# A planned ten-stage transformer kernel: the norms' reciprocal roots move from VectorE chains to two GpSimd instructions each

## Chip, cores and metric

One core of a Trainium2 chip. The time is the device time of one launch in microseconds (us), the median of several runs. TensorE is the matmul engine (PE), VectorE is DVE, ScalarE is ACT, GpSimd is POOL; SyncE (SP) issues nearly all DMAs.

## The reference

Two blocks follow each other on x of 256 rows x 1024 columns, all in float32. Each has two layers. In outline:

```python
def _rmsnorm(x, g):  # over 1024 columns
    y = x * rsqrt(mean(x * x, -1) + EPS)
    return y * g
def _swiglu(x, wg, wu, wd):  # d_ff = 2816
    return (silu(x @ wg) * (x @ wu)) @ wd
# first block, layers 0 (even) and 1 (odd):
x = x + 0.5 * _rmsnorm(_swiglu(_rmsnorm(x, g[0]), ...), g[1])
x = x + _rmsnorm(mixer(_rmsnorm(x, g[2])), g[3])
x = x + 0.5 * _rmsnorm(_swiglu(_rmsnorm(x, g[4]), ...), g[5])
# mixer of layer 0: conv module (31 taps, layer norm) and banded attention; of layer 1: forgetting attention
# second block:
h = x + mlstm_mixer(rmsnorm(x))        # rsqrt of the mean square per head inside
h = h + swiglu(rmsnorm(h))
kv = rmsnorm(h) @ w_kv
h = h + chunked_relpos_attention(rmsnorm(h), kv)
h = h + swiglu(rmsnorm(h))
return rmsnorm(h, final_norm_g)
```

## The kernel before

The ten stages are called F1 (feed-forward), even, F3, F4, fox, F6, ml, F8, rel, F10, and then `final`. x stays in SBUF as two tiles of 128 rows, b0 and b1. All weights (295 MB of loads in all) stream from HBM once, in "units" of 128 x 2048 floats. Each is split by ACT (high part, rounded) and DVE (low part, the rest) into two tiles of the matmul's type, tag `hl`; a product is three matmuls (high x high, high x low, low x high), method `mm3`. Four of the feed-forward stages pair some chunks after Strassen, with additions on DVE.

A norm ahead of a stage (`norm`) multiplies x by the gain on DVE, transposes it on TensorE through PSUM (`split_T`: ACT copies the high half, DVE subtracts for the low half, tag `xt`), and squares x on ACT with a sum over the columns (`ssq`). The root scales the product only afterwards, when its PSUM bank is evacuated. A post-norm (`postnorm`, six stages) squares the accumulator on ACT, takes the product with the gain on DVE, and needs the root before x is updated; the next stage's norm begins with that x.

The root is `rstd`: a chain on DVE that starts from an integer guess and does three Newton steps on a column of 128 x 1 (128 x 4 for the mLSTM heads). It is called 20 times for norms ahead of a projection (with `more=True`, which adds half the root), 12 times for post-norms, twice for the conv's layer norm, four times for the mLSTM heads. `cut=3` lets the planner put other work between its steps. The final norm's two roots go through `pow`: two GpSimd instructions.

All operations are recorded first (`Rec`), each with an assumed duration and a key. `schedule` is a planner inside the program: it picks for each engine the ready operation with the smallest key, hands out tile buffers of a fixed count per tag, and so fixes the order in each queue. `NUDGE` is a table of corrections to the keys, one entry for each labelled group of operations (" p" for its matmuls); it is where the work order is set. DMA loads are ordered in the same way; the first ones (constants, x, the four pieces of weight unit 0) have negative keys. Profile lines name the helper that records the operation: L213 `act`, L223 `tt`, L233 `ts`, L242 `stt`, L293 `mm`, L298 `tr`, L302 `load`, L271 and L273 `pow`.

Of the kernel before, what the change touches and what calls it, by code (L numbers as in the profile page):

```python
# [8 lines left out]
I32 = mybir.dt.int32  # L9
AF = mybir.ActivationFunctionType  # L10
# [66 lines left out]
class Rec:  # L77
# [189 lines left out]
    def pow(self, s, a, b, key=None):  # L267

        v, y, e = s[:, 0:1], s[:, 1:2], s[:, 2:3]
        self.op("POOL", 350, [a, b], [v],  # L270
                lambda: self.nc.gpsimd.tensor_scalar(self.res(v), self.res(a), self.res(b), EPS, ALU.add, ALU.add), key=key)  # L271
        self.op("POOL", 600, [v, e], [y],
                lambda: self.nc.gpsimd.tensor_tensor(self.res(y), self.res(v), self.res(e), ALU.pow), key=key)  # L273
        return y
# [25 lines left out]
    def load(self, out, src, nbytes, key=None, after=None):  # L300
        o = self.op("DMA", max(nbytes / (360.0 if key > 0 else 250.0), 453.0), [src], [out],
                    lambda: self.nc.sync.dma_start(self.res(out), self.res(src)),  # L302
                    lat=4000.0 if nbytes >= 400000 and out.v.name[:3] != "raw" else 2000.0, key=key)
        if after is not None:
            o.deps.append(after)
            after.succ.append(o)
            o.soft = after
        return o
# [180 lines left out]
class Net:  # L489
# [12 lines left out]
    def consts(self):  # L502
# [3 lines left out]
        w = r.t("s", name="warm")  # L506
        r.memset(w[:, 0:1], 0.0, key=-40)
# [6 lines left out]
        for b in range(2):  # L514
            x = r.t("x", name=f"x{b}")
            for h in range(2):
                r.load(x[:, h * 512:(h + 1) * 512], a["x"][b * P:(b + 1) * P, h * 512:(h + 1) * 512], P * 2048, key=-30 + 0.15 * b + 0.75 * h)
            self.x.append(x)
# [60 lines left out]
    def rstd(self, ss, w, n, key, more=False, cut=1):  # L579

        r = self.r
        s = r.t("s", name="rs")
        v, vh, y, t = s[:, 0:w], s[:, w:2 * w], s[:, 2 * w:3 * w], s[:, 3 * w:4 * w]
        r.begin()
        r.ts(v, ss[0], 1.0 / n, EPS, ALU.mult, ALU.add)
        if len(ss) > 1:
            r.end(key)
            r.begin()
            r.stt(v, ss[1], 1.0 / n, v, ALU.mult, ALU.add)
        r.ts(y.bitcast(I32), v.bitcast(I32), -0.5, 1597463007.0, ALU.mult, ALU.add)  # L590
        r.ts(vh, v, -0.5, None, ALU.mult)
        for i in range(3):
            if w == 1:
                r.stt(t, y, vh, y, ALU.mult, ALU.mult)
            else:
                r.tt(t, y, y, ALU.mult)
                r.tt(t, t, vh, ALU.mult)
            r.stt(y, t, 1.5, y, ALU.add, ALU.mult)
            if cut > 1 and i < 2:
                r.end(key)  # L600
                r.begin()
        if more:
            r.stt(s[:, 5:6], y, 0.5, y, ALU.mult, ALU.mult)
            r.ts(s[:, 4:5], y, 0.5, None, ALU.mult)
        r.end(key)
        if more:
            return y, s[:, 4:5], s[:, 5:6]
        return y
# [16 lines left out]
    def ssq(self, b, key):  # L625
# [3 lines left out]
        for h in range(2):  # L629
            junk = r.t("b2", name="junk")  # L630
            r.act(junk[:, :], self.x[b][:, h * 512:(h + 1) * 512], AF.Square, accum=ss[:, h:h + 1], key=key)
# [82 lines left out]
    def postnorm(self, b, acc, g, scale):  # L714
# [5 lines left out]
        for h in range(2):  # L720
            sl = slice(h * 512, h * 512 + 512)
            junk = r.t("b2", name="junk")
            r.act(junk[:, :], acc[h][:, :], AF.Square, accum=ss[:, h:h + 1], key=key)
# [896 lines left out]
    def final(self, gi):  # L1620
        r = self.r
        g = self.gain(gi, self.u - 5)
        for b in range(2):
# [7 lines left out]
            s = r.t("s", name="rs")  # L1631
            r.memset(s[:, 2:3], -0.5, key=key - 40)
            r.tt(y[:, 512:], self.x[b][:, 512:], g[:, 512:], ALU.mult, key=key)
            rs = r.pow(s, ss[:, 0:1], ss[:, 1:2], key=key)
# [26 lines left out]
def arrange(i):  # L1661
# [276 lines left out]
```

## Time and profile before

| | |
|---|---|
| median of 3 runs | 1586.29 us (1584.86 to 1587.45) |
| profiled execution | 1587.08 us, span from first to last instruction 1585.3 us |
| mean granted TensorE clock | 0.997 |
| TensorE busy | 1548.6 us |
| DVE, ACT, GpSimd busy | 1217.4, 938.1, 1.9 us |
| loads and stores | 296.92 MB, 187 GB/s over the span |

A matmul group's busy time counts pipelined instructions that overlap, so the place where TensorE loses time is read from its idle gaps and its granted clock, not from the mean of an instruction.

### The profile page before, as it was taken

To read this page: it belongs to the slowest core of one execution; us is meant where nothing else is said; L and a number is where in the kernel's file an instruction comes from. 1 tells how busy PE (TensorE), PEld (TensorE's weight loads), DVE (VectorE), ACT (ScalarE), POOL (GpSimd) and SP (SyncE) were. 2 spreads that over 40 slices of the span, in tenths; PEclk is the share of its full clock that TensorE was granted. 3 is DMA by queue.
4 is the path that set the end of the run, shared out by engine and by line. 5 is a ranking of instruction groups with operands and counts; after the bars stand their busy time and mean duration, and the time that the engine had idled before them with its cause. 6 is when DMAs were issued, how large, how long until landed. Compare 5 with 4: busy or idle time off the path is not lost.

```text
span 1585.3 us, 21242 instructions
## 1 busy us (share of the span) xinstructions
PE 1548.6 (98%) x7546; PEld 1266.6 (80%) x7546; DVE 1217.4 (77%) x2137; ACT 938.1 (59%) x1480; POOL 1.9 (0%) x8
## 2 busy tenths in 40 slices
PE   8999999999999999999999999999999999999998
PEld 6888878788887888787787887788877887788886
DVE  6555689798878869776899687898788674788784
ACT  6444545865555656456875565656566566765562
POOL 0000000000000000000000000000000000000000
PEclk9999999999999999999999999999999999999999
DMA  8556466447474475643664475455463755464560
GB/s 329 199 186 210 164 219 222 136 169 232 146 269 156 152 242 166 223 155 125 208 207 166 168 259 196 130 184 188 158 212 134 245 174 178 165 216 149 188 231 35
DMA packets 86779, 296.92 MB, mean 187 GB/s; under 512 B 9552, under 2 KB 13072, under 8 KB 86672
## 3 DMA queue, kind: packets, MB, share of 16 engines
q1 hardware_dynamic: 86384, 295.03, 55.1%
q8 instruction: 59, 0.97, 0.2%
q10 hardware_dynamic: 288, 0.52, 0.1%
q14 instruction: 48, 0.39, 0.1%
HBM read 294.44 MB, written 1.08 MB: 186 GB/s over the span
## 4 chain that ended last, share of the span: by engine, by line
PE 90%; DVE 6%; ACT 1%; issue 1%; DMA 1%; SPq 0%; POOLq 0%; POOL 0%; DVEq 0%; ACTq 0%
PE mm L293 59%; PE acc L293 27%; PE mm L298 4%; DVE hl L223 1%; DVE b L242 1%; DVE s L242 1%; ACT b L213 1%; DVE b L223 1%; DMA b<-in_w 1%; DVE x L242 1%; DMA x<-in_x 0%; DVE xt L223 0%; DVE s L233 0%; DVE b L254 0%; ACT L213 0%
## 5 line engine op out<-in xcount | busy, mean ns | idle before, releaser
L293 PE MATMUL mm<-hl,xt 128*128 128x512 f32 (+1 forms) x4104 | 983.6, 393 | 5.6 <-DVE xt L223 1.9
L293 PEld LDWEIGHTS mm<-hl,xt 128*128 128x128 f32 x4104 | 758.1, 188 | 168.7 <-DVE xt L223 4.8
L223 DVE TENSOR_TENSOR hl<-b,hl 128x1024 fp32r<-128x1024 f32 (+1 forms) x554 | 660.7, 1212 | 147.5 <-PE mm L293 70.5
L213 ACT ACTIVATE hl<-b 128x1024 fp32r<-128x1024 f32 (+1 forms) x554 | 572.5, 1052 | 325.4 <-PE mm L293 196.3
L293 PE MATMUL acc<-hl,gt 128*128 128x512 f32 x1584 | 385.7, 393 | 1.2 <-DVE gt L223 0.7
L293 PEld LDWEIGHTS acc<-hl,gt 128*128 128x128 f32 x1584 | 296.8, 189 | 63.9 <-DVE gt L223 1.9
L213 ACT ACTIVATE b<-mm,s 128x256 f32<-128x256 f32 (+2 forms) x150 | 77.3, 520 | 157.6 <-PE mm L293 151.1
L223 DVE TENSOR_TENSOR b<-b,b 128x1024 f32<-128x1024 f32 (+2 forms) x112 | 116.8, 1057 | 10.9 <-DMA b<-in_w 10.1
L298 PE MATMUL mm<-cst,b 128*128 128x128 f32 (+1 forms) x648 | 96.2, 276 | 9.7 <-DVE b L223 4.3
L298 PEld LDWEIGHTS mm<-cst,b 128*128 128x128 f32 (+1 forms) x648 | 77.5, 141 | 32.7 <-DVE b L223 7.0
L242 DVE SCALAR_TENSOR_TENSOR b<-mm,s,b 128x256 f32<-128x256 f32 x102 | 48.9, 479 | 63.2 <-ACT b L213 62.9
L293 PE MATMUL acc<-hl,xt 128*128 128x512 f32 x384 | 93.2, 395 | 0.9 <-DVE hl L223 0.9
L213 ACT ACTIVATE b<-b,s 128x256 f32<-128x256 f32 (+2 forms) x184 | 77.8, 450 | 24.9 <-DVE b L223 14.9
L293 PEld LDWEIGHTS acc<-hl,xt 128*128 128x128 f32 x384 | 70.6, 188 | 17.3 <-DVE hl L223 1.3
L223 DVE TENSOR_TENSOR gt<-mm,gt 128x512 fp32r<-128x512 f32 (+1 forms) x72 | 46.1, 642 | 32.7 <-ACT gt L213 32.4
L213 ACT ACTIVATE gt<-mm 128x512 fp32r<-128x512 f32 (+1 forms) x72 | 39.7, 553 | 41.7 <-PE mm L298 37.8
L213 ACT ACTIVATE b<-mm 128x512 f32<-128x512 f32 (+3 forms) x84 | 45.2, 546 | 13.8 <-PE mm L298 10.7
L242 DVE SCALAR_TENSOR_TENSOR s<-s 128x1 f32<-128x1 f32 (+2 forms) x248 | 45.4, 183 | 7.4
L213 ACT ACTIVATE b<-x 128x512 f32<-128x512 f32 x44 | 27.5, 627 | 25.8 <-DVE x L223 12.4
L242 DVE SCALAR_TENSOR_TENSOR hl<-b,cst,hl 128x512 fp32r<-128x512 f32 x48 | 33.1, 745 | 7.7 <-issue 7.6
L213 ACT ACTIVATE hl<-b,cst 128x512 fp32r<-128x512 f32 x48 | 32.7, 719 | 4.1 <-PE mm L293 3.3
L213 ACT ACTIVATE xt<-mm 128x512 fp32r<-128x512 f32 x40 | 23.4, 593 | 15.8 <-PE mm L298 14.9
(79 smaller groups left out, 597.9 us busy)
## 6 DMA issues: line engine op xcount, KB each, us to landing
b<-in_w SPq DMA_DIRECT2D x512, 512.0 KB, 5.1
g<-in_gains SPq DMA_DIRECT2D x16, 512.0 KB, 6.8
b<-in_diag SPq DMA_DIRECT2D x8, 512.0 KB, 4.6
b<-dr SPq DMA_DIRECT2D x16, 256.0 KB, 5.7
g<-in_relb SPq DMA_DIRECT2D x4, 512.0 KB, 4.7
b<-in_diag SPq DMA_DIRECT2D x4, 448.0 KB, 7.9
x<-in_x SPq DMA_DIRECT2D x4, 256.0 KB, 2.8
b<-in_w SPq DMA_DIRECT2D x4, 256.0 KB, 6.0
```

The costliest lines, as they stand in the source:

```text
L213: return self.nc.scalar.activation(self.res(out), self.res(in_), func, **kw)
L223: lambda: self.nc.vector.tensor_tensor(self.res(out), self.res(a), self.res(b), op), key=key)
L242: lambda: self.nc.vector.scalar_tensor_tensor(self.res(out), self.res(a), self.res(s), self.res(b), op0, op1, **kw), key=key)
L293: lambda: self.nc.tensor.matmul(self.res(out), self.res(l), self.res(r), start=start, stop=stop, **(dict(skip_group_check=True) if again e ...
L298: lambda: self.nc.tensor.transpose(self.res(out), self.res(in_), self.res(ident)), key=key)
```

## The change

`rstd` becomes two GpSimd instructions: the sum of the two half sums (or mean) plus EPS, then a power of -0.5 with a constant tile `mhalf` as exponent; with `more`, a third one halves the root. The division by 1024 moves into the scale of the squares (1/32). `pow` goes, and the final norm calls `rstd` too. The first loads are keyed otherwise: in SP's queue they stood as constants, x0 left, x1 left, weight piece 1, piece 2, x0 right, piece 3, x1 right, piece 4; by the new keys they stand as constants, x0 left, x0 right, piece 1, x1 left, piece 2, x1 right, piece 3, piece 4. The planner's assumed time of a first load, and of a GpSimd instruction, changes as well. The whole table `NUDGE` is replaced, so that every engine's order is another one.

```diff
-    def pow(self, s, a, b, key=None):
...
+    def pts(self, out, a, s1, s2, op0, op1=None, key=None):
...
+            return self.nc.gpsimd.tensor_scalar(*args)
+
+        self.op("POOL", 700, [a, s1, s2], [out], em, key=key)
+
+    def ptt(self, out, a, b, op, key=None):
+        self.op("POOL", 650, [a, b], [out],
+                lambda: self.nc.gpsimd.tensor_tensor(self.res(out), self.res(a), self.res(b), op), key=key)
...
-        o = self.op("DMA", max(nbytes / (360.0 if key > 0 else 250.0), 453.0), [src], [out],
+        o = self.op("DMA", max(nbytes / 360.0 + 0, 453.0), [src], [out],
...
+        self.mhalf = r.t("s", name="mhalf")
+        r.memset(self.mhalf[:, 0:4], -0.5, key=-39)
...
-                r.load(x[:, h * 512:(h + 1) * 512], a["x"][b * P:(b + 1) * P, h * 512:(h + 1) * 512], P * 2048, key=-30 + 0.15 * b + 0.75 * h)
+                r.load(x[:, h * 512:(h + 1) * 512], a["x"][b * P:(b + 1) * P, h * 512:(h + 1) * 512], P * 2048, key=-30 + self.c["xb"] * b + 0.2 * h)
...
-        r.ts(v, ss[0], 1.0 / n, EPS, ALU.mult, ALU.add)
         if len(ss) > 1:
-            r.end(key)
-            r.begin()
-            r.stt(v, ss[1], 1.0 / n, v, ALU.mult, ALU.add)
-        r.ts(y.bitcast(I32), v.bitcast(I32), -0.5, 1597463007.0, ALU.mult, ALU.add)
-        r.ts(vh, v, -0.5, None, ALU.mult)
-        for i in range(3):
...
+            r.pts(v, ss[0], ss[1], EPS, ALU.add, ALU.add, key=key)
+        else:
+            r.pts(v, ss[0], 1.0 / n, EPS, ALU.mult, ALU.add, key=key)
+        r.ptt(y, v, self.mhalf[:, 0:w], ALU.pow, key=key)
         if more:
...
+            r.pts(s[:, 2 * w:2 * w + 1], y, 0.5, None, ALU.mult, key=key)
+            return y, s[:, 2 * w:2 * w + 1]
...
-            r.act(junk[:, :], self.x[b][:, h * 512:(h + 1) * 512], AF.Square, accum=ss[:, h:h + 1], key=key)
+            r.act(junk[:, :], self.x[b][:, h * 512:(h + 1) * 512], AF.Square, scale=1 / 32, accum=ss[:, h:h + 1], key=key)
...
-            s = r.t("s", name="rs")
-            r.memset(s[:, 2:3], -0.5, key=key - 40)
...
-            rs = r.pow(s, ss[:, 0:1], ss[:, 1:2], key=key)
+            rs = self.rstd([ss[:, 0:1], ss[:, 1:2]], 1, D, key)
...
-    "F1 D0 b0 p": -1.5, "F1 D0 b1 p": 5, "F1 D1 b0 p": -5.5, "F1 D1 b1 p": -1.75, "F1 D10 b0 p": -6.5, "F1 D10 b1": 2.25,
+    "F1 D0 b0 p": -9, "F1 D1 b0 p": 4, "F1 D1 b1 p": 3.75, "F1 D10 b0 p": -13.75, "F1 D10 b1": 0.25, "F1 D10 b1 p": 1,
...
```

## Rows read from the trace of the kernel before

**Rows 1.** The page, its first part: busy time, share, instructions of each engine.

```profile
PE 1548.6 (98%) x7546; PEld 1266.6 (80%) x7546; DVE 1217.4 (77%) x2137; ACT 938.1 (59%) x1480; POOL 1.9 (0%) x8
```

**Rows 2.** Waits of TensorE, first and last of 14: us in total, times, longest.

```profile
PE mm L298 <- DMA x<-in_x: 7.0, 2, 4.0
...
PE mm L298 <- ACT b L213: 0.3, 1, 0.3
```

**Rows 3.** Groups by line: two of tiny DVE instructions; count, busy us, mean ns.

```profile
L242 DVE SCALAR_TENSOR_TENSOR s<-s 128x1 f32<-128x1 f32 (+2 forms) x248 | 45.4, 183 | 7.4
...
L233 DVE TENSOR_SCALAR s<-s 128x1 f32<-128x1 f32 (+2 forms) x138 | 17.3, 149 | 1.8 <-ACT s L213 0.4
```

**Rows 4.** Timeline of the first final norm: start us, length us, engine, instruction.

```profile
1573.55 0.69 DVE L223 TENSOR_TENSOR b<-x,g 128x512 f32<-128x512 f32 x1
1574.08 0.19 ACT L213 ACTIVATION_READ_ACCUMULATOR b<-x 128x1 f32 x1
1574.37 0.30 POOL L271 TENSOR_SCALAR s<-s 128x1 f32<-128x1 f32 x1 [1573.94 <-ACT b L213]
1574.75 0.57 POOL L273 TENSOR_TENSOR s<-s 128x1 f32<-128x1 f32 x1
...
1575.36 0.75 DVE L242 SCALAR_TENSOR_TENSOR b<-x,s,g 128x512 f32<-128x512 f32 x1 [1.12 <-POOL s L273]
```

**Rows 5.** Timeline, border of F1 and even; in brackets the idle time before.

```profile
199.25 0.21 ACT L213 ACTIVATION_READ_ACCUMULATOR b<-acc 128x1 f32 x1
...
204.81 1.31 DVE L242 SCALAR_TENSOR_TENSOR s<-s 128x1 f32<-128x1 f32 x6
206.15 1.41 DVE L242 SCALAR_TENSOR_TENSOR x<-b,s,x 128x512 f32<-128x512 f32 x2
...
208.22 1.26 PE L298 MATMUL mm<-cst,b 128*128 128x128 f32 x8 [2.00 <-DVE b L223]
```

**Rows 6.** Timeline, border of F3 and F4.

```profile
480.03 0.19 ACT L213 ACTIVATION_READ_ACCUMULATOR b<-acc 128x1 f32 x1
...
481.30 1.31 DVE L242 SCALAR_TENSOR_TENSOR s<-s 128x1 f32<-128x1 f32 x6
...
483.67 1.41 DVE L242 SCALAR_TENSOR_TENSOR x<-b,s,x 128x512 f32<-128x512 f32 x2
...
485.74 1.26 PE L298 MATMUL mm<-cst,b 128*128 128x128 f32 x8 [0.80 <-DVE b L223]
...
489.21 6.65 PE L293 MATMUL mm<-hl,xt 128*128 128x512 f32 x28 [1.21 <-DVE xt L223]
```

**Rows 7.** Timeline, border of F4 and fox.

```profile
667.72 0.19 ACT L213 ACTIVATION_READ_ACCUMULATOR b<-acc 128x1 f32 x1
...
668.99 1.31 DVE L242 SCALAR_TENSOR_TENSOR s<-s 128x1 f32<-128x1 f32 x6
...
670.77 0.44 PE L298 MATMUL mm<-cst,b 128*128 128x128 f32 x2 [2.22 <-DVE b L242]
...
672.69 1.97 PE L298 MATMUL mm<-cst,b 128*128 128x128 f32 x8 [1.49 <-DVE b L223]
```

**Rows 8.** Windows at that border: busy us of each engine, granted clock, DMA.

```profile
672.00:676.00 4.00, 3.31 (x12) 3.02 (x13) 3.77 (x14) 2.04 (x6) 0.00 (x0) 0.50 0.24 74
676.00:680.00 4.00, 4.00 (x28) 3.27 (x28) 2.26 (x10) 2.23 (x6) 0.00 (x0) 0.74 0.17 61
```

**Rows 9.** Timeline, border of F6 and ml.

```profile
978.74 0.19 ACT L213 ACTIVATION_READ_ACCUMULATOR b<-acc 128x1 f32 x1
...
985.64 0.73 PE L293 MATMUL mm<-hl,xt 128*128 128x512 f32 x2 [0.85 <-ACT xt L213]
```

**Rows 10.** Windows at the start; the last number is GB/s.

```profile
4.00:8.00 4.00, 1.89 (x8) 1.44 (x8) 2.69 (x9) 2.69 (x9) 0.00 (x0) 1.00 0.86 216
8.00:12.00 4.00, 3.05 (x10) 2.61 (x11) 2.38 (x10) 3.71 (x12) 0.00 (x0) 1.00 0.99 368
```

**Rows 11.** Group by line: DVE's low half of the weight splits.

```profile
L223 DVE TENSOR_TENSOR hl<-b,hl 128x1024 fp32r<-128x1024 f32 (+1 forms) x554 | 660.7, 1212 | 147.5 <-PE mm L293 70.5 <-ACT hl L213 32.0 <-PE acc L293 29.5
```

More of the change, by code (lines that the diff above doesn't have):

```diff
@@ L265, in rec, with em @@
                 lambda: self.nc.vector.reciprocal(self.res(out), self.res(a)), key=key)
-    def pow(self, s, a, b, key=None):
[L269 to L274, printed above, removed]
+    def pts(self, out, a, s1, s2, op0, op1=None, key=None):
+        def em():
+            args = [self.res(out), self.res(a), self.res(s1), self.res(s2), op0]
+            if op1 is not None:
+                args.append(op1)
+            return self.nc.gpsimd.tensor_scalar(*args)
[3 more added lines that the diff above has]
+                lambda: self.nc.gpsimd.tensor_tensor(self.res(out), self.res(a), self.res(b), op), key=key)
     def memset(self, out, val, key=None):
@@ L582, in rstd @@
         s = r.t("s", name="rs")
-        v, vh, y, t = s[:, 0:w], s[:, w:2 * w], s[:, 2 * w:3 * w], s[:, 3 * w:4 * w]
-        r.begin()
-        r.ts(v, ss[0], 1.0 / n, EPS, ALU.mult, ALU.add)
+        v, y = s[:, 0:w], s[:, w:2 * w]
         if len(ss) > 1:
-            r.end(key)
-            r.begin()
-            r.stt(v, ss[1], 1.0 / n, v, ALU.mult, ALU.add)
-        r.ts(y.bitcast(I32), v.bitcast(I32), -0.5, 1597463007.0, ALU.mult, ALU.add)
-        r.ts(vh, v, -0.5, None, ALU.mult)
-        for i in range(3):
[L593 to L601, printed above, removed]
-        if more:
[L603 to L607, printed above, removed]
+            r.pts(v, ss[0], ss[1], EPS, ALU.add, ALU.add, key=key)
+        else:
+            r.pts(v, ss[0], 1.0 / n, EPS, ALU.mult, ALU.add, key=key)
+        r.ptt(y, v, self.mhalf[:, 0:w], ALU.pow, key=key)
+        if more:
+            r.pts(s[:, 2 * w:2 * w + 1], y, 0.5, None, ALU.mult, key=key)
+            return y, s[:, 2 * w:2 * w + 1]
         return y
@@ L722, in postnorm @@
             junk = r.t("b2", name="junk")
-            r.act(junk[:, :], acc[h][:, :], AF.Square, accum=ss[:, h:h + 1], key=key)
+            r.act(junk[:, :], acc[h][:, :], AF.Square, scale=1 / 32, accum=ss[:, h:h + 1], key=key)
             r.stt(u[h][:, :], acc[h][:, :], scale, g[:, sl], ALU.mult, ALU.mult, key=key)
@@ L1732 @@
 NUDGE = {
[91 rows of a table removed]
-    "F8 sums": -3.5, "even attn b0": 0.75, "even attn b1": -0.25, "even attn b1 p": -9.25, "even conv": 1,
[10 rows of a table removed]
-    "fox bias3 b1": 2.75, "fox gate b0": -7.75, "fox gate b0 p": -14, "fox gate b1 p": 3.25, "fox norm b0": -0.75,
[54 rows of a table removed]
[90 rows of a table added]
+    "F8 sums": 6.75, "even attn b0": 1.25, "even attn b0 p": 0.75, "even attn b1": -0.25, "even attn b1 p": -12,
+    "even conv": -0.5, "even conv b0": -0.25, "even conv b0 p": 4, "even conv b1": -2.75, "even ln b0 p": 1,
[8 rows of a table added]
+    "fox gate b0 p": -5, "fox gate b1 p": 0.5, "fox norm b0": -3.75, "fox norm b0 p": -4.75, "fox norm b1 p": -13.75,
[53 rows of a table added]
 }
```

304 rows, old and new, of the table NUDGE are left out of this document.

## Prediction

> **What bounds the kernel now.** I read the busy shares first: TensorE is busy for 1548.6 us of a span of 1585.3 us, VectorE (DVE) for 1217.4, ScalarE (ACT) for 938.1, GpSimd (POOL) for 1.9 [rows 1]. The order of matmuls is new but their set is the same, so only what TensorE loses can change: idle time, and time at half clock. Next the waits of TensorE's own queue: fourteen rows that add up to 29.0 us, of which 7.0 are the first load of x and 22.0 lie inside the kernel [rows 2] (the rest of its 36.7 us of idle time, 7.7, lies mostly behind the last matmul). The reader is to see that 22 us is all that this change can win inside, however much work it takes off DVE. Then I followed each place where TensorE stood still in the timeline and asked which engine was late, and whether a root chain stood on that engine just before. Four places have one, all at the borders where a stage's post-norm feeds the next stage's norm: F1 to even, F3 to F4, F4 to fox, F6 to mLSTM [rows 5, 6, 7, 9]. The other waits (attention, silu gates, splits of Strassen weights) have no chain in front.
>
> **What is removed, and what takes its place.** There are 40 norms' roots; the two of the final norm already run on GpSimd. The other 38 (20 norms ahead of a projection, 12 post-norms, 2 of the conv's layer norm, 4 of the mLSTM heads) are chains of 9 to 12 tiny DVE instructions. Nearly all the tiny DVE instructions of the two largest such groups belong to them: 45.4 + 17.3 = 62.7 us busy [rows 3], and smaller groups add a little. So DVE should fall from 1217 to about 1150 us. As DVE isn't the bound, this by itself is worth nothing; it is hidden behind TensorE's matmuls.
>
> In its place come 76 GpSimd instructions and 20 more that halve the root. The final norm shows the price on an idle DVE: the sum of squares is read out by 1574.27 (1574.08 + 0.19), GpSimd takes 0.30 and 0.57 us, and DVE starts with the root at 1575.36: 1.09 us from hand to hand [rows 4]. GpSimd should go to 40 x 0.87 + 20 x 0.30 = about 41 us. The 20 halvings I price at 0.30 each by the same row, hidden, since their users are evacuations after a whole projection. The roots of the mLSTM heads are four wide, which no row shows: between 0.57 and four times 0.57 = 2.3 us, I take 0.6 (one instruction's fixed part being the likelier share), and they are hidden: the product is used only after the o projection. Memset of the constant, scale 1/32 inside the squares, and the tile it holds for good (one of 16 small ones): nothing measurable, as the first lies in DVE's idle start and the second adds no instruction; a lack of small tiles would show up only as another order.
>
> **The four borders.** A DVE chain costs its place in DVE's queue; the pair does not.
>
> F1 to even. The squares were read out by 199.46, but DVE came to the chain late; six of its steps ran 204.81 to 206.12, the update of x followed at 206.15, and the transposes waited 2.00 us until 208.22 [rows 5]. With the pair the root is there at about 199.46 + 1.09 = 200.55, so x is updated as soon as DVE is done with the gains, and the whole chain leaves the path. Six of its ten steps take 1.31 us, all ten some 2; the wait is 2.00. I take 1.9, bounds 0 and 2.0.
>
> F3 to F4. Squares read by 480.22; chain until 482.61, so 2.39 us from the read-out to the root; x at 483.67, as a weight split was queued between [rows 6]. The pair would be ready at 481.31, 1.3 earlier. TensorE's wait of 0.80 goes; the wait of 1.21 for a low half behind it stays, because DVE's splits cause it. I take 0.8, bounds 0 and 2.0 (both waits gone).
>
> F4 to fox. Squares by 667.91, chain until 670.30; TensorE waited 2.22 us for a gate and 1.49 us for the norm's product [rows 7]. The pair is ready at 669.00, 1.3 us earlier, so the second wait goes but for 0.2; the first has another cause and stays. This stall also lowered the clock: granted 0.50 for 672 to 676, that is the lower of the two levels, and 0.74 over 676 to 680 [rows 8]. Of TensorE's busy time there, 3.31 x 0.50 + 4.00 x 0.26 = 2.7 us were lost. Whether a shorter stall keeps the clock up no row says; I take half, 1.3, bounds 0 and 2.7. Together 1.3 + 1.3 = 2.6.
>
> F6 to mLSTM. Squares by 978.93, TensorE waited 0.85 us for the high half of the transposed product at 985.64 [rows 9]; the pair is ready 1.3 us earlier here too. I take 0.8, bounds 0 and 0.85.
>
> **Loads and order.** The first loads: x's second block of rows moves behind the first weight piece, and x's second half of the first rows ahead of it; the first weight piece stays fourth in SP's queue, the second goes from fifth to sixth, the third from seventh to eighth. So transposes of the first rows start earlier and the second weight piece lands one load later. A load of 256 KB takes 0.7 us at 368 GB/s and 1.2 at 216 GB/s [rows 10], so the start moves by at most 1.2 either way; I take 0, as one engine wins about what the other loses. No other DMA changes its queue; POOL's queue holds nothing but the roots, so a root can only wait for an earlier root.
>
> The work order is made anew throughout. Of the 22.0 us inside, the four borders hold 2.00 + 0.80 + 1.21 + 3.71 + 0.85 = 8.6; the rest, 13.4, is dealt again. I take the same sum, with 4 us either way (a third of it).
>
> **The sum.** 1.9 + 0.8 + 2.6 + 0.8 = 6.1 us. The profiled execution took 1587.08 us, 1.8 more than its span and 0.8 more than the median of the three; 1587.1 - 6.1 = 1581.0, and on the median's footing 1580.2. With all upper bounds the sum is 2.0 + 2.0 + 1.5 + 2.7 + 0.85 = 9.05, and with 4 more from the new order 1573.2.
>
> **The rivals.**
>
> GpSimd and DVE hinder each other (slower). DVE's commonest instruction takes two inputs from SBUF, 1.21 us each, 660.7 us in all, 42% of the span [rows 11]. If each of the pair must first let such an instruction end, the pair takes 0.22 + 0.30 + 0.57 + 2 x 1.21 = 3.5 us from the read-out, against the chain's 2.4, and DVE's own queue is held up by the pair's 0.87. At the three borders where the squares come last, x is then 1.1 + 0.9 = 2.0 us later each: 6 us, 1592. It decides once a pair takes over 2.4 us; from some 3.4 on the three cost more than 0.2%. For it: no row speaks against the price, as nothing in this trace shows a GpSimd instruction beside such a DVE instruction, since the last DVE one ended at 1574.24, before GpSimd began [rows 4]. Against: at those borders DVE's own instruction at that moment is the product of the accumulator with the gain, which has one input in PSUM; and the chain's absence frees DVE. Chance 0.09. The Trainium skill says just this: in "SBUF — State Buffer", under Who interferes with whom, a DVE instruction with two SBUF inputs and a GpSimd instruction that reads SBUF exclude each other for their whole length; by that the result would be this rival's. No row here bears it out or denies it.
>
> The new order has dry places of its own (slower). One more stall like that of F4 to fox costs 3.7 idle and 2.7 at half clock, 6.4 us, and eats the gain: 1586.4. Two make 1592.8. For it: 13.4 of the 22.0 us inside have nothing to do with roots and follow only from the order. Against: in the four borders shown only one has such a stall now. Two or more: 0.12.
>
> The gain is taken back (no change). At the borders ACT's high half and DVE's low half still stand behind weight splits, so TensorE waits a little later for those, or one dry place appears: 1584 to 1588. For it: at F3 to F4 the longest wait, 1.21 us, is for a low half behind splits [rows 6]. Chance 0.24.
>
> **How the numbers follow.** Forecast 0.55, no change 0.24, slower 0.09 + 0.12 = 0.21. A measurement of this kernel tells about 0.2%, 3.2 us, from no change: so faster 0.55, same 0.24, slower 0.21. The forecast alone spans 1573 to 1583. The range takes in no change and half of the slower cases: 1573 to 1591.
>
> **What would show it.** GpSimd near 41 us in about 104 instructions; the 248 tiny DVE instructions down to a couple of dozen; the power instruction still near 0.57 us (0.8 or more would show the hindrance, a DVE split well over 1.21 us likewise); TensorE's waits for the norm's product gone at the four borders, and the granted clock 1.00 through F4 to fox; TensorE's waits inside near 15 us. The prediction is wrong if the waits of rows 2 come back at other places, if a second stretch shows a clock below 1, or if a pair takes 2.4 us and more from the read-out.

## The result, and the profile after

The changed kernel takes 1563.65 us (median of 3 runs, 1561.65 to 1565.78) against 1586.29: a ratio of 0.9859, 95% interval 0.9839 to 0.9878. That is 22.6 us faster, where the prediction had 6.1 and a range from 1573 to 1591. The profiled execution took 1565.78 us.

The page after, its span and the first part (busy us, share of the span, instructions), as in [rows 1]:

```profile
span 1564.0 us, 20954 instructions
...
PE 1540.0 (98%) x7546; PEld 1266.3 (81%) x7546; DVE 1163.0 (74%) x1710; ACT 938.8 (60%) x1480; POOL 68.6 (4%) x104
```

The span is 21.3 us shorter: TensorE stands still 12.7 us less (36.7 to 24.0) and is busy 8.6 us less (1548.6 to 1540.0) with the same 7546 matmuls. DVE lost 54 us and is at 1163, near the 1150 foreseen; GpSimd has the 104 instructions foreseen, but 68.6 us in place of 41.

The waits of TensorE after (us in total, times, longest), which answer to [rows 2], the first four and the last of 12:

```profile
PE mm L302 <- DMA x<-in_x: 4.4, 2, 4.0
PE mm L302 <- DVE hl L223: 2.8, 1, 2.8
PE mm L297 <- DVE b L223: 2.4, 2, 2.2
PE mm L297 <- ACT xt L213: 1.5, 2, 1.2
...
PE mm L297 <- ACT b L213: 0.3, 1, 0.3
```

They add up to 16.4 us; the first two are the start (7.2), so 9.2 lie inside, against 22.0 before. The largest one inside, 2.2 us, is new and lies in F10.

Both traces have the same matmuls, so I took their start times at equal shares of TensorE's work and subtracted. At the start the new kernel has won 0; around the border F1 to even 3.2 to 3.7; within even 4.4; around F3 to F4 4.9; around F4 to fox 4.9; within fox 2.4; around F6 to ml it loses some 0.3; in F8 it wins 1.8, up to F10 2.4 more, and at the new stall of F10 it loses 3.8. These make 20 of the 21.3 us. The trace of the control below, the same kernel once more, gives the same places to within 1 us but for two: it loses 1.1 us at the start, and in F10 only 0.8.

The border F3 to F4 after, from the timeline (start us, length us, engine, instruction, idle time before it), which answers to [rows 6]:

```profile
466.00 8.44 PE L297 MATMUL acc<-hl,gt 128*128 128x512 f32 x36
...
469.52 0.19 ACT L213 ACTIVATION_READ_ACCUMULATOR b<-acc 128x1 f32 x1
...
469.81 0.30 POOL L272 TENSOR_SCALAR s<-s 128x1 f32<-128x1 f32 x1 [166.00 <-ACT b L213]
...
470.19 0.57 POOL L278 TENSOR_TENSOR s<-s,s 128x1 f32<-128x1 f32 x1
470.39 1.23 DVE L223 TENSOR_TENSOR hl<-b,hl 128x1024 fp32r<-128x1024 f32 x1
...
471.53 0.74 DVE L242 SCALAR_TENSOR_TENSOR x<-b,s,x 128x512 f32<-128x512 f32 x1
...
474.28 1.03 PE L302 MATMUL mm<-cst,b 128*128 128x128 f32 x8
...
475.07 3.00 PE L297 MATMUL acc<-hl,gt 128*128 128x512 f32 x12
```

Two things differ from [rows 6]. The pair ran unhindered, 0.30 and 0.57 us, while a weight half ran on DVE in the 1.2 us in which the chain used to stand there. And the planner kept back twelve matmuls of the other rows' down-projection (`x12` at 475.07): TensorE has them to do while ACT and DVE make the halves of the transposed product. Before, all of them stood in front of the transposes, and TensorE waited 0.80 and 1.21 us.

At F4 to fox the clock is kept. Windows (length, busy us of PE, PEld, DVE, ACT, POOL, granted clock, DMA share, GB/s), which answer to [rows 8]:

```profile
656.00:660.00 4.00, 4.00 (x23) 3.36 (x22) 4.00 (x7) 3.68 (x8) 0.80 (x1) 1.00 0.41 147
660.00:664.00 4.00, 2.75 (x21) 1.81 (x20) 4.00 (x6) 3.12 (x8) 3.38 (x5) 1.00 0.74 240
664.00:668.00 4.00, 4.00 (x33) 3.27 (x31) 3.39 (x9) 2.12 (x6) 1.51 (x4) 1.00 0.43 158
```

TensorE still loses 1.25 us in the second window, mostly one wait of 1.15 us for the copies of xt, but the clock stays at 1.00 where it was 0.50 before.

### The profile page after: what moved, and what is told of

It reads as the page before. It is cut to its first block, busy times and chain, and to the rows that moved or that the text cites. A ratio compares the mean times of both kernels' runs of the same rounds, so it can differ in the third digit from the quotient of the medians.

```text
span 1564.0 us, 20954 instructions
## 1 busy us (share of the span) xinstructions
PE 1540.0 (98%) x7546; PEld 1266.3 (81%) x7546; DVE 1163.0 (74%) x1710; ACT 938.8 (60%) x1480; POOL 68.6 (4%) x104
## 4 chain that ended last, share of the span: by engine, by line
PE 91%; DVE 4%; ACT 2%; DMA 1%; issue 1%; SPq 0%; POOL 0%; POOLq 0%; ACTq 0%; DVEq 0%
PE mm L297 60%; PE acc L297 27%; PE mm L302 4%; DVE hl L223 2%; DMA b<-in_w 1%; ACT hl L213 1%; DVE b L242 1%; ACT b L213 1%; DVE b L223 0%; DMA x<-in_x 0%; DVE b L254 0%; SPq L306 0%; DVE xt L223 0%; DVE gt L223 0%; DVE x L242 0%
## 5 line engine op out<-in xcount | busy, mean ns | idle before, releaser
L223 DVE TENSOR_TENSOR hl<-b,hl 128x1024 fp32r<-128x1024 f32 (+1 forms) x554 | 660.7, 1213 | 165.6 <-PE mm L297 76.3
L272 POOL TENSOR_SCALAR s<-s 128x1 f32<-128x1 f32 (+1 forms) x60 | 40.3, 673 | 1487.5 <-ACT b L213 1402.0
L213 ACT ACTIVATE b<-b,s 128x128 f32<-128x128 f32 (+2 forms) x184 | 77.6, 450 | 26.3 <-DVE b L223 14.8
L223 DVE TENSOR_TENSOR xt<-mm,xt 128x512 fp32r<-128x512 f32 x40 | 26.9, 686 | 12.7 <-ACT xt L213 8.7
```

The costliest lines, as they stand in the source:

```text
L213: return self.nc.scalar.activation(self.res(out), self.res(in_), func, **kw)
L223: lambda: self.nc.vector.tensor_tensor(self.res(out), self.res(a), self.res(b), op), key=key)
L272: return self.nc.gpsimd.tensor_scalar(*args)
```

## The experiments

Ratios are to the kernel before on the same chip. The comments in the diffs are explanations and no part of the kernels. The unedited new kernel ran again as a yardstick (`e5_control_new`); experiments of other batches are set beside one another by their ratios.

**Order and roots apart.** `e1_new_plan_dve_roots`: the new kernel, with DVE's chain emitted at the place of each pair.

```diff
+        for o, f in zip(r.ops[first:], (one, two, three)):
+            o.em = [f]  # the recorded GpSimd operations emit the old chain on DVE, in three parts
```

> The changed kernel's order on TensorE, ACT and SyncE, instruction for instruction; only the 38 + 2 roots go back to DVE, as a chain at the place that the pair had. Theory 'roots' (the pair itself gives the gain, at the borders): most of the 22.6 us comes back, 1578 to 1588 us, TensorE's waits inside return to about 20 us. Theory 'order' (the new work order gives it): 1564 to 1571 us. If both are needed together: between, 1571 to 1578.

Measured: 1610.38 us, ratio 1.015 (1.0135 to 1.0165), so slower than before and outside both theories. Its waits of TensorE for DVE, the four longest rows:

```profile
PE mm L297 <- DVE xt L223: 13.3, 9, 4.7
PE mm L302 <- DVE b L223: 7.4, 8, 2.2
...
PE mm L297 <- DVE hl L223: 5.2, 4, 1.7
PE mm L302 <- DVE b L242: 5.1, 6, 1.5
```

Most of these stand at stage borders. The chains stand here at places where the planner had put none. An order planned with a new table and the chains was not run, so this shows that this order does not bear the chains, not that no new order could win with them.

`e2_old_plan_pool_roots`: the kernel before, every engine's order kept, the pair emitted where the chain began.

```diff
+        for o in r.ops[first:]:
+            o.em = []
+        r.ops[first + (len(ss) > 1)].em = [pair]
```

> The order of the kernel before on TensorE, ACT and SyncE, instruction for instruction; only the 38 roots leave DVE for the pair on GpSimd. Theory 'roots': 1564 to 1575 us. Theory 'order': 1580 to 1586 us. My prediction's own sum for the four borders alone was 6.1 us, 1580.2; a result there would say that the borders were sized rightly and the rest is the order.

Measured: 1583.65 us, ratio 0.9973 (0.9963 to 0.9983): in the range of the theory 'order', and under the 6.1 us that the prediction had for the borders. At F1 to even it wins 2.8 us by 206 us, and has lost 2.9 again by 214. The transposes start without a wait, but then TensorE waits 1.7 us for ACT's copies of xt, which stand in ACT's queue behind the squares of x, and the granted clock falls (0.72 and 0.85 in the two windows of 4 us from 208). Waits for these copies, in the kernel before and here:

```profile
PE mm L293 <- ACT xt L213: 1.1, 2, 0.8
...
PE mm L293 <- ACT xt L213: 2.8, 3, 1.7
```

So the roots in the old order win some 4 us of the 22.6, and the new order with the chains loses some 24; only together do they win.

**First loads.** `e3_new_but_old_first_loads`: the new kernel with the first loads issued in the old order.

```diff
+        for i, j in zip(at, (0, 1, 4, 3, 5, 2, 7, 6, 8)):
+            self.order[i] = first[j]  # the first nine DMAs, put back
```

> The changed kernel with its first nine loads issued in the order of the kernel before, all else as it is. By my sum 0, bounds 1.2 us either way: 1562 to 1566. The rival that the first loads matter: beyond 1.2 us, seen in TensorE's start.

Measured: 1566.15 us, ratio 0.9867 (0.9851 to 0.9884): the interval overlaps that of the new kernel. In its profile 2.4 us are lost in the first 150 matmuls; but the control, with the new loads, starts 1.1 us later than the first profile too. So the loads are worth between nothing and some 2 us.

**Does GpSimd hold up DVE?** `e4_idle_pool_work`: one idle power instruction on GpSimd beside each weight unit.

```diff
+        r.ops[-1].em.append(lambda: r.nc.gpsimd.tensor_tensor(idle[:, 8:9], idle[:, 0:1], idle[:, 4:5], ALU.pow))
```

> The changed kernel with one idle power instruction more on GpSimd for each weight unit (some 260, on tiles of its own; most run in bursts behind a norm's roots, beside the weight splits). Theory 'one-sided' (a GpSimd instruction that reads SBUF waits for DVE's two-input instructions, DVE waits for nothing): the mean of DVE's splits stays at 1.21 to 1.23 us, the idle instructions that meet a split take 1 to 3 us, time within 0.3% of 1563.7. Theory 'both block' (whichever starts first holds the other up for its whole length): splits beside a burst grow by up to 0.57 us, DVE's busy time by 50 us or more, time 1570 or more.

Measured: 1565.99 us, ratio 0.9871 (0.9856 to 0.9885), no change that can be told. The group of idle instructions (count, busy us, mean ns, idle before):

```profile
L581 POOL TENSOR_TENSOR idle<-idle 128x1 f32<-128x1 f32 x219 | 167.8, 766 | 14.9
```

They take 766 ns on the mean, not 570, but DVE's weight halves still take 1213 ns each. A mean could hide a few cases. Of the new kernel's 92 GpSimd instructions on 128 x 1, 30 begin while DVE runs an instruction of 512 columns or more with both inputs in SBUF; all 30 take longer than their usual 0.19 to 0.30 or 0.57 us, from 0.45 to 2.78. The other 62 take 0.61 us at most. The other way round, 23 weight halves begin while a GpSimd instruction is under way, and take 1.21 to 1.23 us like the rest; in ten of these cases the GpSimd instruction keeps its length too. At these sizes GpSimd waits for DVE, and DVE does not wait for GpSimd.

**Which roots.** The control, the 12 post-norms' roots put back as chains (and the two of the final norm, which the condition takes in as well), and the 20 roots of the norms at a stage's head put back as chains, all in the new order:

```diff
+        for o, f in zip(r.ops[first:], (one, two, three) if len(ss) > 1 and not more else ()):  # e6
...
+        for o, f in zip(r.ops[first:], (one, two, three) if more else ()):  # e7
```

> The changed kernel again, unedited, on the chip of the next three kernels, to be their yardstick: 1561 to 1567 us by every theory. Its F10 stage has a wait of TensorE near 1514 us from the start in every profile so far (2.17 in the first, 1.9 and 1.1 in those of two variants); if it is the order's and not chance it is there again, with 1 to 2.2 us.

> The new work order, with DVE's chain in the place of the GpSimd pair for the 12 norms behind a feed-forward or mixing stage alone (the ones whose root stands between the read-out and the next stage's transposes); the other 28 roots stay on GpSimd. Theory 'border', the prediction's: these are the roots that TensorE waits for, so nearly the whole loss of the kernel with all chains back (1610, 44 us over) comes with them: 1590 to 1608 us. Theory 'queue': a chain costs by what stands behind it in DVE's own order, wherever it is; these 12 hold about a third of the 61 us that the chains take on DVE, so about a third of the loss: 1574 to 1584 us.

> The new work order, with DVE's chain in the place of the GpSimd pair for the 20 norms at the head of a stage alone (the ones that the prediction put down as hidden, since their scale is wanted only at the gates); the other 20 roots stay on GpSimd. Theory 'border': hidden, so no more than 3 us over the control: 1563 to 1568 us. Theory 'queue': the chains stand in DVE's order ahead of the halves and gates of the stage's first units, and two thirds of the 61 us of chains are theirs: 1585 to 1600 us.

Measured: control 1564.57 (ratio 0.985, 0.9835 to 0.9865); post-norms 1582.35 (0.9961, 0.9947 to 0.9976), 17.8 us more; norms 1585.78 (0.9984, 0.9974 to 0.9995), 21.2 us more. Both lie in the ranges of the theory 'queue' and outside those of 'border'. The 20 roots that the prediction called hidden cost 1.1 us each, not much less than the 14 others with 1.3, of which 0.8 us in all lie behind the last matmul. The border F6 to ml shows how. TensorE in the control:

```profile
966.14 1.03 PE L302 MATMUL mm<-cst,b 128*128 128x128 f32 x8
967.57 0.74 PE L297 MATMUL mm<-hl,xt 128*128 128x512 f32 x2 [0.39 <-ACT xt L213]
969.31 1.20 PE L297 MATMUL mm<-hl,xt 128*128 128x512 f32 x4 [1.00 <-DVE xt L223]
```

TensorE and DVE with the norms' chains:

```profile
981.21 0.74 PE L297 MATMUL mm<-hl,xt 128*128 128x512 f32 x2 [0.39 <-ACT xt L213]
...
982.23 0.22 DVE L611 SCALAR_TENSOR_TENSOR s<-s 128x1 f32<-128x1 f32 x1
...
983.38 0.16 DVE L615 SCALAR_TENSOR_TENSOR s<-s 128x1 f32<-128x1 f32 x1
983.45 0.69 DVE L242 SCALAR_TENSOR_TENSOR b<-acc,g 128x512 f32<-128x512 f32 x1
984.05 0.68 DVE L223 TENSOR_TENSOR xt<-mm,xt 128x512 fp32r<-128x512 f32 x1
...
984.79 2.07 PE L297 MATMUL mm<-hl,xt 128*128 128x512 f32 x4 [2.85 <-DVE xt L223]
```

Nobody needs this root soon. But its chain (from 981.98) stands in DVE's queue ahead of the low half `xt` that TensorE does need, and the wait grows from 1.00 to 2.85 us. Behind it four matmuls take 2.07 us in place of 1.20, since the granted clock fell to 0.50 as well; windows of that kernel:

```profile
980.00:984.00 4.00, 1.55 (x10) 0.88 (x8) 3.68 (x13) 3.53 (x7) 1.94 (x2) 0.94 0.44 152
984.00:988.00 4.00, 3.21 (x17) 2.64 (x18) 3.99 (x9) 1.34 (x4) 0.00 (x0) 0.50 0.26 84
988.00:992.00 4.00, 4.00 (x26) 3.32 (x24) 3.35 (x16) 0.00 (x0) 0.00 (x0) 0.71 0.41 131
```

In the control the same border keeps 1.00. A wait that grows by 1.85 us thus costs 4.3 us by the matmuls' start times there.

**A stall of the new kernel mended.** In F10 of the profiled execution ACT stood at a weight transfer, and DVE's gate, two weight halves and the emptying of a bank queued behind. The timeline:

```profile
1508.12 2.01 ACT L213 ACTIVATE hl<-b 128x1024 fp32r<-128x1024 f32 x2 [2.44 <-DMA b<-in_w]
1510.03 0.49 ACT L213 ACTIVATE b<-b,s 128x256 f32<-128x256 f32 x1
...
1510.56 0.48 DVE L242 SCALAR_TENSOR_TENSOR b<-b,s,b 128x256 f32<-128x256 f32 x1 [3.67 <-ACT b L213]
...
1513.23 0.68 DVE L223 TENSOR_TENSOR b<-mm,b 128x512 f32<-128x512 f32 x1
...
1514.06 6.15 PE L297 MATMUL mm<-hl,xt 128*128 128x512 f32 x19 [2.17 <-DVE b L223]
```

Behind the wait the granted clock was lower too, so that 3.8 us were lost by a wait of 2.17; windows:

```profile
1512.00:1516.00 4.00, 1.94 (x5) 1.59 (x6) 3.42 (x5) 1.87 (x3) 0.00 (x0) 0.75 0.60 198
1516.00:1520.00 4.00, 4.00 (x16) 3.26 (x15) 2.91 (x4) 2.12 (x2) 0.00 (x0) 0.82 0.83 267
```

`e8_new_without_late_split` puts that weight half behind the silu.

```diff
+        i = next(i for i, o in enumerate(q) if (o.lab, o.eng, o.n) == ("unit255", "ACT", 4413))
+        j = next(j for j, o in enumerate(q) if (o.lab, o.eng, o.n) == ("F10 W7d", "ACT", 4354))
+        q.insert(j, q.pop(i))
```

> The changed kernel with one ScalarE instruction, a weight's high half of a later unit in F10 whose transfer comes late, put three instructions further down in ScalarE's order, behind the silu that DVE's next instruction waits for. Theory 'in order': the wait near 1514 us comes from ScalarE standing at that transfer (2.44 us idle) with DVE's gate, two halves and the emptying of a bank behind it; the wait (1.1 to 2.2 us) and the stretch at half clock behind it go: 2 to 4 us under the control, 1560 to 1562 us. Rival 'transfer': the late transfer itself is the bound, TensorE meets it a few us later: within 1 us of the control.

Measured: 1563.68 us (1562.73 to 1564.20), control 1564.57 (1563.61 to 1565.43); ratios 0.9844 (0.9829 to 0.9859) and 0.985. The wait is gone, and TensorE does not meet the late transfer later, so the rival's mechanism is out. But in the control the wait was only 0.7 us long, without a fall of the clock; at that place the trace wins 1.1 us (1.6 in all). The times differ by 0.9 us with overlapping ranges, under the 2 to 4 expected: likely better, not shown.

**The places at one border.** Three first attempts left a load or a copy out of step with the instruction that was moved; a moved weight half waited for, and was made from, the next load's data, and in the second the copies read the banks ahead of the transposes. Their times settle nothing: 1584.73, 1564.52 and 1589.66 us.

> The old plan with the roots on GpSimd (as the second experiment, 1583.65), and at the border F3 to F4 alone four instructions put where the new plan has them: the last twelve matmuls of the other rows' down-projection behind the eight transposes of F4's first rows, not in front; a weight half on DVE behind the x updates and the gains, not in front; and the read-out of those twelve behind the copies of the transposes. Theory 'places': with the chain gone from DVE the x updates can follow the root at once, and the twelve matmuls fill the wait for the halves; of the waits that the second experiment has at this border (0.53, 0.18, 0.29 and 1.20 us) 1 to 2 us go and the time is 1581.5 to 1583. Rival 'the whole order': one border by hand gains nothing, since the gain is handed back at the next wait: 1583 to 1585, and the lead over the second experiment is gone within 30 us behind the border.

> The changed kernel with the twelve matmuls at F3 to F4 put back in front of the eight transposes, nothing else. Theory 'places': the eight transposes start about 3 us later without a wait, and then TensorE waits for the copies and halves of xt with nothing to fill it: 1 to 2.5 us more, 1565 to 1567 us. Rival 'slack': the halves come early enough in the new order, and the place of the twelve is worth under 0.5 us: 1563.5 to 1565.

> The kernel before, chains on DVE, with the same four instructions moved at F3 to F4 as in the ninth. Theory 'places': the root is ready about 1.6 us later than from GpSimd, TensorE waits 2 us or more ahead of the eight transposes, since only 24 matmuls are left in front of them, and the move is worth 0 to 1 us, less than with the roots on GpSimd: 1585 to 1587 if before's median here is 1586 to 1588. Rival 'order alone': the move gains as much with the chain on DVE as without it, 1 to 2 us.

With loads and copies moved along: `e12_old_plan_pool_hand_move2` (old order, roots on GpSimd), `e13_new_filler_in_front2` (new kernel, the other way), `e14_before_hand_move2` (the kernel before).

```diff
+        behind(1337, 1311, 1312)   # e12, e14: PE, the last 12 matmuls behind the 8 transposes
+        behind(1336, 1380, 1445)   # DVE, a weight half (and its tile's next load) behind x and x*gain
+        behind(1340, 1390, 1446, 1392, 1457)   # two more halves and loads behind the halves of xt
+        behind(1339, 1322)         # ACT, the read-out of the 12 behind the four copies
...
+        behind(1309, 1329, 1334)   # e13: the 8 transposes behind the 12 matmuls
+        behind(1334, 1330, 1331, 1335, 1336)   # and their copies
```

> The ninth again, with what hangs on the moved instructions moved along: in the ninth and the eleventh the moved weight half reads its tile only after the next load into it, and in the tenth the four copies read the transposes' banks ahead of the transposes, so that these three waited for other things than their edit says (and computed with other data). Old plan, roots on GpSimd, the four moves at F3 to F4 of the ninth, and two weight halves on DVE with their tiles' loads behind the two halves of xt. Theory 'places': 1 to 2 us better at the border than the second experiment, whose waits there are 0.53, 0.18, 0.29 and 1.20 us; time 1581.5 to 1583. Rival 'the whole order': the lead is gone within 30 us, 1583 to 1585.

> The tenth again, with the copies moved along: the changed kernel, the eight transposes and their four copies at F3 to F4 behind the last twelve matmuls of the other rows' down-projection. Theory 'places': TensorE then waits for the copies and the halves of xt with nothing to fill it, 1 to 2.5 us more: 1565 to 1567 us. Rival 'slack': under 0.5 us, 1563.5 to 1565.

> The eleventh again with the loads moved along: the kernel before, chains on DVE, the moves of the twelfth. Theory 'places': the move is worth 0 to 1 us, less than with the roots on GpSimd: 1585 to 1588 beside a median of before of 1586 to 1589. Rival 'order alone': as much as in the twelfth, 1 to 2 us.

Measured: 1581.63 (ratio 0.9957, 0.9941 to 0.9974), 1565.52 (0.9856, 0.9842 to 0.9871) and 1588.83 (1.0003, 0.9994 to 1.0013). The times say only that the move did not help the kernel before: the twelfth's interval overlaps that of the second run, and the thirteenth's that of the control. What the move did at the border is in the traces, one execution of each kernel. TensorE with the old order and GpSimd roots, before the move:

```profile
476.89 8.43 PE L293 MATMUL acc<-hl,gt 128*128 128x512 f32 x36
485.85 1.26 PE L298 MATMUL mm<-cst,b 128*128 128x128 f32 x8 [0.53 <-DVE b L223]
487.40 0.73 PE L293 MATMUL mm<-hl,xt 128*128 128x512 f32 x2 [0.29 <-ACT xt L213]
489.32 3.10 PE L293 MATMUL mm<-hl,xt 128*128 128x512 f32 x7 [1.20 <-DVE xt L223]
```

after the move:

```profile
476.59 5.71 PE L293 MATMUL acc<-hl,gt 128*128 128x512 f32 x24
483.46 1.32 PE L298 MATMUL mm<-cst,b 128*128 128x128 f32 x8 [1.15 <-DVE b L223]
484.54 3.02 PE L293 MATMUL acc<-hl,gt 128*128 128x512 f32 x12
487.39 4.92 PE L293 MATMUL mm<-hl,xt 128*128 128x512 f32 x21
```

and after the same move in the kernel before, with the chain:

```profile
477.29 5.71 PE L293 MATMUL acc<-hl,gt 128*128 128x512 f32 x24
485.51 1.97 PE L298 MATMUL mm<-cst,b 128*128 128x128 f32 x8 [2.50 <-DVE b L223]
487.13 3.77 PE L293 MATMUL acc<-hl,gt 128*128 128x512 f32 x12
```

By the matmuls' start times the move wins 2.9 us at the border with GpSimd roots and loses 2.6 with the chain. With the chain the root is late, 24 matmuls do not last until it comes, TensorE waits 2.50 us in one piece, and then the granted clock is down to 0.57 over 4 us; window of that kernel:

```profile
485.00:489.00 4.00, 3.49 (x13) 3.16 (x14) 3.12 (x5) 3.57 (x7) 0.00 (x0) 0.57 0.12 37
```

The eleventh run, with the same places on TensorE, shows the same wait of 2.50 us in its trace and loses 2.1. But the profiled execution of the fourteenth is the slowest of its ten (1591.99), and the interval of its ratio reaches from a gain of 1.0 us to a loss of 2.1: that the move hurts with the chain is read from traces, and the times show only that it doesn't help.

In the new kernel, undoing the twelve matmuls' place loses 1.9 us at the border, of which 0.9 is left at the end, as in the times: between the two theories.

**Time on DVE or lateness of the root.** `e15_idle_chains_on_dve`: the new kernel, its roots from GpSimd, and beside each pair eight idle DVE instructions (eleven at the four of 128 x 4) at the chain's place.

```diff
+        r.ops[-1].em.append(chain)   # eight tiny DVE instructions on a scratch tile
```

> The changed kernel, roots on GpSimd as they are, and beside each of the 40 power instructions eight idle instructions on DVE of the chain's form (on a scratch tile, waiting for nothing and awaited by nothing) at the chain's place in DVE's order. Theory 'DVE time': a chain costs by the 1.5 us that it holds DVE in front of the halves, gates and gains, whoever makes the root: 1590 to 1610 us, most of the 44 us of the first experiment. Rival 'latency': what costs is that the root comes later and that DVE stands waiting for the sum of squares; idle instructions cost little: 1565 to 1578 us.

Measured: 1597.69 us, ratio 1.0056 (1.0041 to 1.0071). DVE is 49 us busier and the kernel 33 us slower than the control (1564.57), though every root comes from GpSimd. First row of its waits:

```profile
PE mm L297 <- DVE xt L223: 9.9, 7, 4.0
```

So of the 47 us that the first experiment lost against the control, 33, some 70%, come with time in DVE's queue alone. The real chains held DVE longer, for 61 us more than the pairs do, so their share may be larger; the rest is left for the root's lateness and DVE's waiting for the squares, which no run separates.

## Why the prediction was wrong

**The step that failed** is "The work order is made anew throughout ... I take the same sum", together with "As DVE isn't the bound, this by itself is worth nothing". Both terms were treated as additive and small. They are neither: old order with chains 1, old order with pairs 0.9973, new order with chains 1.015, new order with pairs 0.9859. The new order leaves the chains no room in DVE's queue and uses it for weight halves, gains and the halves of xt; at F1 to even and F3 to F4 it also has twelve matmuls left behind the transposes. At one border the places were set by hand: in the traces they win 2.9 us with pairs and lose 2.6 with chains. That the other borders work alike is read from the waits of the first, sixth, seventh and fifteenth runs; they were not rebuilt one by one. How much a new order planned with the chains would have won stays open.

**"Hidden" roots.** The 20 norms' roots were left at nothing because their users come late. In the new order their chains cost 21.2 us, more than the 17.8 of the post-norms' on the path (and the final norm's). The price was in DVE's order: what stands behind the chain, not who waits for its result. I looked for waits with a chain just in front in the old order, which was planned with the chains in it; this showed what chains cost there (about 4 us, second run), not what an order without them could do.

**"22 us is all that this change can win inside"** counted idle time alone. The gain happens to stay near it, but is made otherwise: the span lost 12.7 us of idle time and 8.6 of busy time, which the ceiling leaves out. About 1.6 of the 8.6 is clock, an estimate worked out from the windows as in the prediction: 2.8 us of busy time were lost to it before (the 2.7 of F4 to fox, and 0.1 in the window ahead of these), 1.2 after (1.94 x 0.25 + 4.00 x 0.18 in F10). Another part is that a group of matmuls behind a wait takes longer: in [rows 6] the eight transposes took 1.26 us behind a wait, now 1.03 without one. How the rest is made up was not followed.

**The four borders** hold 13 of the 20 us located; the rest lies in even, fox, F8 and what follows, where the prediction had no change. All four are outside their bounds: F1 to even 1.9 against some 3.5, F3 to F4 0.8 against 4.9, F4 to fox 2.6 against 4.9, F6 to ml 0.8 against about -0.3. At F3 to F4 the wait of 1.21 us, said to stay "because DVE's splits cause it", went. Only part of that is due to the twelve matmuls now in front of it: with them put back (thirteenth run) it is 0.48. At F4 to fox the first wait of 2.22 us, "another cause and stays", went too.

**Right:** the pair's price at the borders (0.57 us, and 0.30 at nine of the twelve post-norms, 0.46 to 0.76 at three), DVE near 1150 us (1163), the first loads near nothing, the clock kept through F4 to fox. The power instruction of the four-wide roots, taken as 0.6, measured 1.0 to 2.0 us, with no wait of TensorE beside it in the control.

**The rivals.** The hindrance between GpSimd and DVE is there, but on one side: of 60 GpSimd tensor_scalar instructions the median takes 0.30 us and the longest 2.78. The one at 474.13 begins while DVE takes x times the gain, and two weight halves follow on DVE before it ends:

```profile
474.13 2.78 POOL L272 TENSOR_SCALAR s<-s 128x1 f32<-128x1 f32 x1 [3.37 <-ACT b L213]
...
474.39 2.35 DVE L223 TENSOR_TENSOR hl<-b,hl 128x1024 fp32r<-128x1024 f32 x2
```

This is a norm's root, whose user comes late; at the borders DVE reads PSUM at that moment, as argued. DVE's halves went from 1212 to 1213 ns. The Trainium skill's "SBUF — State Buffer", under Who interferes with whom, says that a DVE instruction with two SBUF inputs contends with a GpSimd instruction that reads SBUF, and calls the lock between them exclusive. The trace agrees where GpSimd's instruction is the later one, and disagrees where DVE's is: in the border shown above the power instruction begins at 470.19, DVE's weight half at 470.39, and both keep their lengths, 0.57 and 1.23 us.

One dry place of the new order came, in F10, with a stretch of lower clock, which the prediction had named as a sign against it; it cost 3.8 us in that execution and 0.8 in the control's, and did not eat the gain. That the gain is taken back is what the second run shows for pairs in the old order, at F1 to even; in the new order it was not. In the sum for that dry place the prediction was 0.2 us short: 1580.2 and 6.4 make 1586.6.

## What to carry to other kernels

A small serial chain on an engine with 25% idle time is not free: price it by what stands behind it in that engine's order and by whether TensorE has work of its own meanwhile. Here moving it off paid little until the order was made anew, and the order made for its absence was worse than the old one with it; so test both together, and judge the order by running it with the old operations too. When waits are summed for a ceiling, add the longer groups of matmuls behind them and the clock.

## What had not been expected of the hardware

GpSimd instructions of 128 x 1 elements stretch up to ninefold (0.30 to 2.78 us) when they begin beside DVE instructions with two SBUF inputs, and the DVE instructions do not stretch at all: 219 more GpSimd instructions, 168 us of them, left DVE's mean at 1213 ns and the time at 1565.99 us. Whether larger GpSimd instructions would hold DVE up, no run here shows.
